# Giving each store of a preparation stage a place of its own among the projection matmuls

## The chip, the cores and the metric

The kernel runs on one core of one Trainium2 chip. The metric is the device time of one execution in microseconds (us); lower is better. Times of a kernel are given as the median of several runs. A profile is one execution recorded by the hardware profiler.

## The reference

One layer of a streaming encoder, for 512 tokens and 16 meta tokens (L = 528) of width 2048. All is float32.

```python
hn = _rmsnorm(h_res, norm_in_g[l])
P = hn @ w_in[l]                      # 2048 x 8320: r, k, v, g_r, lora | B, C, h, g_c
...
# group A: RWKV-7, 16 heads x 64, after a token shift of its columns
kk = (k * k_k[l]).reshape(bsz, L, H, N); kk = kk / norm(kk)
def step(S, inp):
    sa = jnp.einsum('bhvk,bhk->bhv', S, kk_t)
    S = (S * w_t[:, :, None, :] - sa[..., None] * b_t[:, :, None, :]
         + v_t[..., None] * k_t[:, :, None, :])
    y_t = jnp.einsum('bhvk,bhk->bhv', S, r_t)
...
y_a = (yn + bonus) * jax.nn.silu(g_r)                             # yn: GroupNorm of y
y_b = Bg * _causal_depthwise_conv(Cg * hc, conv_w[l]) * jax.nn.silu(g_c)   # group B
h_res = h_res + jnp.concatenate([y_a, y_b], axis=-1) @ w_out[l]
out = _rmsnorm(h_res, norm_f_g)                                   # meta tokens dropped
```

## The kernel before

**Projection.** The input projection is cut into 65 tiles of 128 output columns; `plan` (L105) lists them: lora, then for pair after pair of heads k, r, v, then g, C, h, B, gc. `main` (L323) is a generator that yields after each matmul, so that other work can be put between its matmuls. Full precision is kept by splitting every weight tile into a high and a low part: `prefetch` (L130) requests the 512 KB of half a tile (wr) on SyncE's queue, ScalarE casts it to the high part (wh, L126), and VectorE or GpSimd subtracts to give the low part (wl, L127). Three matmuls (high x high, high x low, low x high) then run per 128 rows. There are three wr buffers and six each of wh and wl.

**Preparation.** `prepare(i)`, for each of the 8 pairs of heads, turns k, r, v and the low-rank paths into the operands of a chunked form of the recurrence (9 chunks of 64 frames): ar, bk, the gram products gt (L625, masked by VectorE at L635), the transposes bt (L655) and vs. A small triangular system per chunk has to be inverted: its blocks go through DRAM (sg, L689) to another layout (d, L697), with the norms beside them (sn, L685, read back as nd, L698), VectorE inverts 16x16 blocks in a chain of some thirty small steps (the y chain, L701 to L734), y goes back through DRAM (sx, L749), and is loaded as xT and xo (L740, L741). `invert` joins two pairs on TensorE. All operands are stored to DRAM tensors opd by `stash` (L567): ar, gt (as O_KK and O_BR), bt (as O_B and O_K), vs (eight stores) and xT. They are read back chunk by chunk (ct, L870) only in `recur`, after all eight pairs. rbd (the bonus), gated (silu of g) and mixd (group B's result) are also stored, and read back by `split_mix` before the output projection (L1070), which takes the last 180 us or so.

**Order.** TensorE's order is written out by hand: the code calls `fill(ns)`, which takes matmuls of the projection from the generator until they fill that much time, and `until(...)`. The order on the other engines and on SyncE's queue is decided by a scheduler with a cost model, from the order of the program, dependences and priorities. `later(ns, fn)` (L482) puts a piece of work on a list that is due when the projection has run `ns` further; `run_pending` issues what is due, under `tc.issue_after(state["dma"])`, which keeps it on SyncE's queue behind the weight request that was issued last.

All these transfers are issued from one queue, SyncE's, in order; a request that waits holds up those behind it.

Of the kernel before, what the change touches and what calls it, by code (L numbers as in the profile page):

```python
# [18 lines left out]
P = 128  # L19
# [5 lines left out]
CH = 64  # L25
NCH = SEQ // CH + 1
# [12 lines left out]
O_AR, O_KK, O_BR, O_X, O_V, O_B, O_K = 0, 128, 256, 320, 384, 448, 512  # L39
# [37 lines left out]
def hymba_kernel(ctx: ExitStack, tc: tile.TileContext, xt, xtok, w_in, w_out, pv, lup, cst, msk, gf, out):  # L77
    nc = tc.nc
# [13 lines left out]
    rbd = [dp.tile([P, SEQ], F32, tag=f"rbd{j}", name=f"rbd{j}", bufs=1) for j in range(NPAIR)]  # L92
    gated = [dp.tile([P, SEQ], F32, tag=f"gated{j}", name=f"gated{j}", bufs=1) for j in range(NPAIR)]
    yd = dp.tile([2 * NPAIR * CH, SEQ], F32, tag="yd", name="yd", bufs=1)
    mixd = {j: dp.tile([P, SEQ], F32, tag=f"mixd{j}", name=f"mixd{j}", bufs=1) for j in range(NPAIR, KT)}
# [25 lines left out]
    state = {"next": 0}  # L121
# [255 lines left out]
    def use(what, i, ps):  # L377
        if what == "lora":
            use_lora(ps)
        elif what in ("k", "v"):  # L380
            t = cq.tile([P, LP], F32, tag=what, name=f"{what}{i}")
            nc.gpsimd.memset(t[:, META:CH], 0.0)
            shift_full(ps, tile_of[what] + i, f"{what}{i}", padded(t))
            got[what, i] = t
        elif what in ("r", "g"):
            t = cq.tile([P, SEQ], F32, tag=f"r{i % 2}" if what == "r" else "g", name=f"{what}{i}")
            shift_real(ps, tile_of[what] + i, f"{what}{i}", t)
            if what == "g":
                gate(t, f"r{i}")
                later(6000, lambda: nc.sync.dma_start(gated[i], t))  # L390
            got[what, i] = t
        elif what == "C":
            u = tm(f"u{i}")
            scaled(TAIL, ps, u, 14)
            got[what, i] = u
        elif what == "h":
            u = got["C", i]
            hh = tm(f"hh{i}")
            scaled(TAIL, ps, hh, 14)
            n = SEQ + 2  # L400
            nc.gpsimd.tensor_tensor(out=u[:, 0:n], in0=u[:, 0:n], in1=hh[:, 0:n], op=ALU.mult)
            cv = tp.tile([P, SEQ], F32, tag="cw", name=f"cv{i}")
            nc.scalar.activation(cv, u[:, 0:SEQ], AF.Copy, scale=col(V_CW, i))
            for j in (1, 2):
                nc.vector.scalar_tensor_tensor(
                    out=cv, in0=u[:, j : j + SEQ], scalar=col(V_CW, 8 * j + i), in1=cv, op0=ALU.mult, op1=ALU.add
                )
            got[what, i] = cv
        elif what == "B":
            cv = got["h", i]  # L410
            b = tm(f"b{i}")[:, 0:SEQ]
            scaled(REAL, ps, b, META)
            nc.gpsimd.tensor_tensor(out=cv, in0=cv, in1=b, op=ALU.mult)
        else:
            cv = got["h", i]
            g = tm(f"gc{i}")[:, 0:SEQ]
            scaled(REAL, ps, g, META)
            gate(g, f"c{i}")
            nc.vector.scalar_tensor_tensor(out=cv, in0=cv, scalar=0.5, in1=g, op0=ALU.mult, op1=ALU.mult)
            nc.sync.dma_start(mixd[8 + i], cv)  # L420
        ready.add((what, i))

    ready = set()
# [58 lines left out]
    def later(ns, fn):  # L482
        pending.append((clock[0] + ns, fn))
        pending.sort(key=lambda e: e[0])

    def run_pending(upto):
        while pending and pending[0][0] <= upto:
            fn = pending.pop(0)[1]
            with tc.issue_after(state["dma"]):
                fn()  # L490

    def step():
        t = next(flow, None)
        if t is None:
            run_pending(float("inf"))
        else:
            clock[0] += t
            run_pending(clock[0])
        return t
# [11 lines left out]
    def until(*key):  # L511
        while key not in ready:
            step()
# [41 lines left out]
    heads = [(h, slice(64 * h, 64 * h + 64), slice(64 - 64 * h, 128 - 64 * h)) for h in range(2)]  # L555
# [10 lines left out]
    def stash(i, src, o, n, row=0, rows_n=P, c0=0, cn=NCH, step=1):  # L566
        nc.sync.dma_start(spot(i, row, rows_n, c0, cn, step, o, n), src)  # L567

    def prepare(i):
        p = i % 2  # L570
        until("k", i)
        k = got["k", i]
        ar = cq.tile([P, NCH, 2, CH], F32, tag="ar", name=f"ar{i}")
# [32 lines left out]
        r = got["r", i]  # L606
# [13 lines left out]
        gt = cq.tile([P, 2, NCH, P], F32, tag=f"gt{p}", name=f"gt{i}")  # L620
# [56 lines left out]
        sx = scr_x[i % 2]  # L677

        def rows(t, h):
            return bass.AP(tensor=t.tensor, offset=t.offset + h * 4 * BLK, ap=[[CH, CH], [8 * BLK, NCH], [1, CH]])  # L680

        def blocks(t):
            return bass.AP(tensor=t.tensor, offset=t.offset, ap=[[BLK, 8 * NCH], [CH, 16], [1, 16]])

        nc.sync.dma_start(  # L685
            bass.AP(tensor=sn.tensor, offset=sn.offset, ap=[[CH, 2], [P, NCH], [1, CH]]), c3(n2[0:2])
        )
        for h in range(2):
            nc.sync.dma_start(rows(sg, h), gt[64 * h : 64 * h + 64, h, :, 0:CH])  # L689
        NB = 8 * NCH  # L690
        d = cq.tile([NB, 256], F32, tag="d", name=f"d{i}").rearrange("p (s t) -> p s t", t=16)
        stash(i, ar.rearrange("p c a s -> p c (a s)"), O_AR, 2 * CH)
        for h, hs, ho in heads:
            stash(i, gt[ho, h], O_KK, 2 * CH, 64 * h, 64)
            stash(i, gt[hs, h, :, CH:P], O_BR, CH, 64 * h, 64)
        nd = cq.tile([NB, 16], F32, tag="nd", name=f"nd{i}")
        nc.sync.dma_start(d, blocks(sg))  # L697
        nc.sync.dma_start(nd, sn.rearrange("(p s) -> p s", s=16))  # L698
        y = cq.tile([NB, 256], F32, tag="y", name=f"y{i}").rearrange("p (s t) -> p s t", t=16)
        nc.gpsimd.memset(y, 0.0)  # L700
        nc.vector.tensor_scalar(out=nd, in0=nd, scalar1=1e-24, scalar2=None, op0=ALU.max)  # L701
# [44 lines left out]
                    ),  # L746
                )

        later(13500 if p else 29000, lambda: nc.sync.dma_start(blocks(sx), y))  # L749
        later(16500 if p else 33000, load_inverse)  # L750

        for h, hs, ho in heads:
            stash(i, bt[hs, h], O_B, CH, 64 * h, 64, 0, NCH - 1)
            stash(i, bt[ho, h], O_K, CH, 64 * h, 64, 0, NCH - 1)
        until("v", i)
        v = got["v", i]
        nc.vector.tensor_tensor(out=r, in0=r, in1=v[:, CH:LP], op=ALU.mult)
        nc.sync.dma_start(rbd[i], r)
        fill(FW["v"])

        vs = cq.tile([P, NCH, CH], F32, tag="vs", name=f"vs{i}")
        nc.vector.transpose(vs.rearrange("p c s -> p (c s)"), v)
        for b in range(4):
            for t in range(2):
                stash(
                    i, vs[32 * b : 32 * b + 32, :, 32 * t : 32 * t + 32], O_V + 32 * (b % 2), 32,
                    64 * (1 - b // 2) + 32 * t, 32,
                )
        fill(FW["vt"])
# [2 lines left out]
    def invert(two):  # L772
# [81 lines left out]
        for q in both:  # L854
            for e in range(2):
                for h, lo, hi in quads:
                    nc.vector.tensor_copy(two[q]["xT"][lo, 2 - e : NCH : 2, 32:CH], z[e][lo, q])
        for t in two:
            if t["i"] % 2 == 0:
                stash(t["i"], t["xT"], O_X, CH)  # L860
            else:
                for h, hs, ho in heads:
                    stash(t["i"], t["xT"][hs], O_X, CH, 64 - 64 * h, 64)
        fill(FW["out"] if first < NPAIR - 2 else FW["begin"])

    def load_chunk(ch, c, pairs, ops):
# [128 lines left out]
    for i in range(0, NPAIR, 2):  # L995
        invert([prepare(i), prepare(i + 1)])
    until("g", NPAIR - 1)
    ph2.close()
    with tc.tile_pool(name="ch", bufs=1, side="right", reuse_waits="tile") as ch:
        recur(ch)  # L1000
# [5 lines left out]
    def split_mix(j):  # L1006
        parts[j] = [pp.tile([P, SEQ], F32R, name=f"m{a}{j}") for a in range(2)]
        mh, ml = parts[j]
        raw = pp.tile([P, SEQ], F32, tag="mraw", name=f"mr{j}", bufs=4)
        if j < NPAIR:  # L1010
            rb = pp.tile([P, SEQ], F32, tag="rb", name=f"rb{j}", bufs=3)
            gg = pp.tile([P, SEQ], F32, tag="gg", name=f"gg{j}", bufs=3)
            nc.sync.dma_start(rb, rbd[j])
            nc.sync.dma_start(gg, gated[j])
            for h, hs, ho in heads:
                o = ((1 - h if place[j] == NPAIR - 1 else h) * NPAIR + place[j]) * CH
                nc.sync.dma_start(raw[hs], yd[o : o + CH])

            for x, w, z, o in ((raw, 0, rb, ALU.mult), (raw, 1, gg, ALU.add)):
                nc.vector.scalar_tensor_tensor(  # L1020
                    out=raw, in0=x, scalar=hl[:, w, j : j + 1], in1=z, op0=o, op1=(ALU.add, ALU.mult)[w]
                )
        else:
            nc.sync.dma_start(raw, mixd[j])
        nc.scalar.copy(mh, raw)
        nc.vector.tensor_tensor(out=ml, in0=raw, in1=mh.bitcast(F32), op=ALU.subtract)
# [8 lines left out]
    for j in range(NPAIR + 4, KT):  # L1035
        while ("gc", j - NPAIR) not in ready:
            step()
        split_mix(j)
    for _ in flow:
        pass  # L1040
# [194 lines left out]
```

## Time and profile before

| | us |
|---|---|
| median of 3 runs | 1056.24 (1056.13 to 1057.02) |
| the profiled execution | 1054.6 |
| its span, first to last instruction | 1052.8 |
| TensorE busy | 1034.8 |
| VectorE busy | 566.4 |
| ScalarE busy | 365.9 |
| GpSimd busy | 308.3 |

The profile's rows name the engine (PE is TensorE, DVE VectorE, ACT ScalarE, POOL GpSimd, SPq SyncE's queue of DMA requests), the line of the kernel, what is written and what is read (out<-in), shapes, and how many instructions are merged in the row. The ends of matmuls are modelled, so a row of TensorE can overlap the next.

The stretches: startup to about 44 us, preparation and inversion of the pairs beside the projection to about 640, the recurrence beside the rest of the projection to about 800, the last of the projection to 865, the output projection to 1040, and the end.

### The profile page before, as it was taken

How to read it: one execution, taken by the hardware profiler on the slowest of the kernel's cores; microseconds unless marked ns; L12 is line 12 of the kernel's file. 1: busy time of each engine (PE TensorE's matmuls, PEld its weight loads, DVE VectorE, ACT ScalarE, POOL GpSimd, SP SyncE). 2: the span in 40 equal slices, each digit the busy share in tenths (PEclk: the TensorE clock that was granted, in tenths of full speed). 3: DMA queues.
4: the chain of work that ended last, by engine and by line, in shares of the span. 5: the costliest groups of instructions: out<-in, count | busy, mean ns of one | idle time of the engine just before them, and what ended most of it. 6: DMA issues, size and time to landing. Idle time of an engine off the chain costs nothing.

```text
span 1052.8 us, 23986 instructions
## 1 busy us (share of the span) xinstructions
PE 1034.8 (98%) x9973; PEld 945.1 (90%) x9973; DVE 566.4 (54%) x1072; ACT 365.9 (35%) x682; POOL 308.3 (29%) x315
## 2 busy tenths in 40 slices
PE   7999999999999999999999999999999999999996
PEld 6999998999998999989999989888898988888885
DVE  6774965559563658653757642455454781212132
ACT  7543422433332433233443232222222342323232
POOL 0132413324222323132323231323233242424232
PEclk9999999999999999999999999999999999999999
DMA  8446475364854363753364748778654978322314
GB/s 297 135 124 155 121 175 142 108 153 120 197 152 115 108 164 112 175 155 114 104 170 127 178 129 291 232 214 248 181 146 112 275 233 302 98 87 95 100 61 160
DMA packets 182893, 167.49 MB, mean 159 GB/s; under 512 B 120960, under 2 KB 143232, under 8 KB 182400
## 3 DMA queue, kind: packets, MB, share of 16 engines
q1 hardware_dynamic: 182208, 164.90, 53.7%
q8 instruction: 78, 1.28, 0.5%
q10 hardware_dynamic: 576, 1.07, 0.3%
q14 instruction: 31, 0.25, 0.1%
HBM read 129.05 MB, written 36.88 MB: 158 GB/s over the span
## 4 chain that ended last, share of the span: by engine, by line
PE 90%; DVE 4%; issue 2%; DMA 1%; ACT 1%; POOL 1%; SPq 0%; DVEq 0%; ACTq 0%; POOLq 0%
PE o L1070 17%; PE ps_g L315 9%; PE ps_gc L315 9%; PE ps_k L315 9%; PE ps_B L315 8%; PE ps_h L315 8%; PE ps_C L315 8%; PE ps_r L315 7%; PE ps_v L315 7%; PE g L625 2%; PE zs L939 1%; PE ps_lora L315 1%; PE rz L889 1%; PE zy L943 1%; DMA wq<-in_w_in_dram 1%
## 5 line engine op out<-in xcount | busy, mean ns | idle before, releaser
L127 POOL TENSOR_TENSOR wl<-wr,wh 128x512 fp32r<-128x512 f32 x150 | 211.2, 1410 | 456.2 <-ACT wh L126 423.2
L126 ACT CAST wh<-wr 128x512 fp32r<-128x512 f32 x312 | 188.7, 619 | 385.2 <-PE o L1070 92.2
L127 DVE TENSOR_TENSOR wl<-wr,wh 128x512 fp32r<-128x512 f32 x162 | 124.8, 775 | 241.4 <-ACT wh L126 236.0
L1070 PE MATMUL o<-wh,m 128*128 128x512 f32 (+1 forms) x484 | 145.3, 384 | 0.0
L1070 PEld LDWEIGHTS o<-wh,m 128*128 128x128 f32 x484 | 89.6, 188 | 21.3
L1070 PE MATMUL o<-wl,m 128*128 128x512 f32 (+1 forms) x242 | 92.6, 389 | 0.0
L315 PE MATMUL ps_k<-xl,wh 128*128 128x264 f32 x256 | 73.2, 286 | 0.0
L315 PE MATMUL ps_g<-xh,wl 128*128 128x258 f32 (+1 forms) x256 | 72.2, 282 | 0.9 <-DVE wl L127 0.8
L315 PE MATMUL ps_v<-xh,wh 128*128 128x264 f32 x256 | 73.1, 286 | 0.0
L315 PE MATMUL ps_k<-xh,wh 128*128 128x264 f32 x256 | 73.0, 285 | 0.0
L315 PE MATMUL ps_r<-xh,wh 128*128 128x258 f32 (+1 forms) x256 | 72.2, 282 | 0.7 <-ACT wh L225 0.7
L315 PE MATMUL ps_h<-xh,wl 128*128 128x258 f32 (+1 forms) x256 | 72.8, 285 | 0.0
L315 PE MATMUL ps_k<-xh,wl 128*128 128x264 f32 x256 | 72.7, 284 | 0.0
L315 PE MATMUL ps_v<-xh,wl 128*128 128x264 f32 x256 | 72.7, 284 | 0.0
L315 PE MATMUL ps_v<-xl,wh 128*128 128x264 f32 x256 | 72.7, 284 | 0.0
L315 PE MATMUL ps_g<-xl,wh 128*128 128x258 f32 (+1 forms) x256 | 72.4, 283 | 0.0
L315 PE MATMUL ps_h<-xh,wh 128*128 128x258 f32 (+1 forms) x256 | 72.3, 282 | 0.0
L315 PE MATMUL ps_g<-xh,wh 128*128 128x258 f32 (+1 forms) x256 | 72.3, 282 | 0.0
L315 PE MATMUL ps_C<-xh,wh 128*128 128x258 f32 (+1 forms) x256 | 72.3, 282 | 0.0
L315 PE MATMUL ps_C<-xh,wl 128*128 128x258 f32 (+1 forms) x256 | 72.3, 282 | 0.0
L315 PE MATMUL ps_r<-xl,wh 128*128 128x258 f32 (+1 forms) x256 | 72.1, 282 | 0.0
L315 PE MATMUL ps_h<-xl,wh 128*128 128x258 f32 (+1 forms) x256 | 72.1, 282 | 0.0
(271 smaller groups left out, 2705.9 us busy)
## 6 DMA issues: line engine op xcount, KB each, us to landing
wr<-in_w_in_dram SPq DMA_DIRECT2D x127, 512.0 KB
ct<-opd SPq DMA_DIRECT2D x64, 288.0 KB
wr<-in_w_out_dram SPq DMA_DIRECT2D x32, 512.0 KB
opd<-ar SPq DMA_DIRECT2D x8, 576.0 KB
opd<-gt SPq DMA_DIRECT2D x16, 288.0 KB
opd<-bt SPq DMA_DIRECT2D x32, 128.0 KB
xres<-in_xtok_dram SPq DMA_DIRECT2D x4, 768.0 KB
out_dram<-xres SPq DMA_DIRECT2D x6, 512.0 KB
```

What stands on the lines that cost most here:

```text
L126: nc.scalar.copy(hi, rq)
L127: eng.tensor_tensor(out=lo, in0=rq, in1=hi.bitcast(F32), op=ALU.subtract)
L315: nc.tensor.matmul(ps[r], ww[:, w], xx[:, kt, a:b], start=(kt == 0 and n == 0), stop=(kt == KT - 1 and n == 2))
L625: nc.tensor.matmul(z[h][:, c - c0], bk[hs, c, h : h + 2, :].rearrange("p a s -> p (a s)"), ar[hs, c].rearrange("p a s -> p (a s)"), start= ...
L889: nc.tensor.matmul(z[e][ho if e else hs, 0, k], t[hs, o : o + CH], t[hs, O_V : O_V + CH] if part else st[hs, 4 * e + k], start=(part == 0 ...
L939: nc.tensor.matmul(d[hs, j], t[hs, o : o + CH], x[hs], start=(a == 0), stop=(a == b - 1))
L943: nc.tensor.matmul(d[ho, j], t[hs, o : o + CH], x[hs], start=(a == 0), stop=(a == b - 1))
L1070: nc.tensor.matmul(ps[t + p], mm[:, tk], ww[:, o], start=(jj == 0 and q == 0), stop=(jj == KT - 1 and q == 2))
```

## The change

Every store of the preparation that went out where its data is produced gets a due time in the run of the projection (`stash_later`, `later`), so that it goes out behind the weight requested last by then. The solver's inputs (sg, sn, d, nd) are issued at once, but under `issue_after` (`behind`): they keep behind the weights requested before them. The write of y and the load of xT of odd pairs are due 7 and 6 us of projection later. The stores of xT (`put_inverse`), gated and mixd are due later too, and two calls of `run_pending` issue what is left before the recurrence and before the last loads of mixd.

```diff
-                later(6000, lambda: nc.sync.dma_start(gated[i], t))
+                later(14000, lambda: nc.sync.dma_start(gated[i], t))
...
-            nc.sync.dma_start(mixd[8 + i], cv)
+            later(9000, lambda: nc.sync.dma_start(mixd[8 + i], cv))
...
+    def behind(dst, src):
+        with tc.issue_after(state["dma"]):
+            nc.sync.dma_start(dst, src)
+    def stash_later(ns, *a):
+        later(ns, lambda: stash(*a))
...
-        nc.sync.dma_start(
+        behind(
             bass.AP(tensor=sn.tensor, offset=sn.offset, ap=[[CH, 2], [P, NCH], [1, CH]]), c3(n2[0:2])
         )
         for h in range(2):
-            nc.sync.dma_start(rows(sg, h), gt[64 * h : 64 * h + 64, h, :, 0:CH])
+            behind(rows(sg, h), gt[64 * h : 64 * h + 64, h, :, 0:CH])
...
-        stash(i, ar.rearrange("p c a s -> p c (a s)"), O_AR, 2 * CH)
+        stash_later(1500, i, ar.rearrange("p c a s -> p c (a s)"), O_AR, 2 * CH)
         for h, hs, ho in heads:
-            stash(i, gt[ho, h], O_KK, 2 * CH, 64 * h, 64)
-            stash(i, gt[hs, h, :, CH:P], O_BR, CH, 64 * h, 64)
+            stash_later(2500 + 1000 * h, i, gt[ho, h], O_KK, 2 * CH, 64 * h, 64)
+            stash_later(4500 + 1000 * h, i, gt[hs, h, :, CH:P], O_BR, CH, 64 * h, 64)
...
-        nc.sync.dma_start(d, blocks(sg))
-        nc.sync.dma_start(nd, sn.rearrange("(p s) -> p s", s=16))
+        behind(d, blocks(sg))
+        behind(nd, sn.rearrange("(p s) -> p s", s=16))
...
-        later(13500 if p else 29000, lambda: nc.sync.dma_start(blocks(sx), y))
-        later(16500 if p else 33000, load_inverse)
+        later(20500 if p else 29000, lambda: nc.sync.dma_start(blocks(sx), y))
+        later(22500 if p else 33000, load_inverse)
         for h, hs, ho in heads:
-            stash(i, bt[hs, h], O_B, CH, 64 * h, 64, 0, NCH - 1)
-            stash(i, bt[ho, h], O_K, CH, 64 * h, 64, 0, NCH - 1)
+            stash_later(6500 + 1000 * h, i, bt[hs, h], O_B, CH, 64 * h, 64, 0, NCH - 1)
+            stash_later(8500 + 1000 * h, i, bt[ho, h], O_K, CH, 64 * h, 64, 0, NCH - 1)
...
-        nc.sync.dma_start(rbd[i], r)
+        later(12500, lambda: nc.sync.dma_start(rbd[i], r))
...
-                stash(
-                    i, vs[32 * b : 32 * b + 32, :, 32 * t : 32 * t + 32], ...
+                stash_later(
+                    14000 + 1000 * (2 * b + t), i, vs[32 * b : 32 * b + 32, :, 32 * t : 32 * t + 32], ...
...
+        def put_inverse():
+            for t in two:
+                ...  # the stores of xT, as before
+        later(5500, put_inverse)
...
     until("g", NPAIR - 1)
+    run_pending(float("inf"))
...
+        run_pending(float("inf"))
         split_mix(j)
```

More of the change, by code (lines that the diff above doesn't have):

```diff
@@ L764, in prepare @@
             for t in range(2):
-                stash(
-                    i, vs[32 * b : 32 * b + 32, :, 32 * t : 32 * t + 32], O_V + 32 * (b % 2), 32,
+                stash_later(
+                    14000 + 1000 * (2 * b + t), i, vs[32 * b : 32 * b + 32, :, 32 * t : 32 * t + 32], O_V + 32 * (b % 2), 32,
                     64 * (1 - b // 2) + 32 * t, 32,
@@ L857, in invert @@
                     nc.vector.tensor_copy(two[q]["xT"][lo, 2 - e : NCH : 2, 32:CH], z[e][lo, q])
[L858 to L863, printed above, removed]
+        def put_inverse():
+            for t in two:
+                if t["i"] % 2 == 0:
+                    stash(t["i"], t["xT"], O_X, CH)
+                else:
+                    for h, hs, ho in heads:
+                        stash(t["i"], t["xT"][hs], O_X, CH, 64 - 64 * h, 64)
+        later(5500, put_inverse)
         fill(FW["out"] if first < NPAIR - 2 else FW["begin"])
```

## The prediction

> **What bounds the kernel now.** I read the page first: span, busy shares, the chain that ended last.
>
> ```profile
> span 1052.8 us, 23986 instructions
> ...
> PE 1034.8 (98%) x9973; PEld 945.1 (90%) x9973; DVE 566.4 (54%) x1072; ACT 365.9 (35%) x682; POOL 308.3 (29%) x315
> ...
> PE 90%; DVE 4%; issue 2%; DMA 1%; ACT 1%; POOL 1%; SPq 0%; DVEq 0%; ACTq 0%; POOLq 0%
> ```
>
> TensorE is busy for 98% of the span and carries 90% of the chain. The order of TensorE's instructions is written by hand and is, instruction for instruction, the same in the changed kernel. So no edit to a store can shorten TensorE's work; it can only remove, or add, pauses in it. I therefore went through TensorE's timeline start by start, from 44 us (the startup is over) to 640 us (the recurrence begins), which is the stretch in which the moved stores lie, and kept every place where the next start is late for its shape. There are four:
>
> ```profile
> 157.87 0.40 PE L315 MATMUL ps_B<-xh,wh 128*128 128x512 f32 x1
> 158.10 0.39 PE L315 MATMUL ps_B<-xl,wh 128*128 128x512 f32 x1
> 159.43 0.50 PE L315 MATMUL ps_B<-xh,wl 128*128 128x512 f32 x1 [0.94 <-DVE wl L127]
> ...
> 255.85 0.28 PE L315 MATMUL ps_g<-xh,wh 128*128 128x258 f32 x1
> 255.97 0.28 PE L315 MATMUL ps_g<-xl,wh 128*128 128x258 f32 x1
> 256.64 0.39 PE L315 MATMUL ps_g<-xh,wl 128*128 128x258 f32 x1 [0.39 <-DVE wl L127]
> 256.87 0.29 PE L315 MATMUL ps_g<-xh,wh 128*128 128x258 f32 x1
> ...
> 408.75 0.28 PE L315 MATMUL ps_g<-xl,wh 128*128 128x258 f32 x1
> 409.41 0.39 PE L315 MATMUL ps_g<-xh,wl 128*128 128x258 f32 x1 [0.38 <-DVE wl L127]
> ...
> 561.72 0.28 PE L315 MATMUL ps_g<-xl,wh 128*128 128x258 f32 x1
> 562.14 0.39 PE L315 MATMUL ps_g<-xh,wl 128*128 128x258 f32 x1
> ```
>
> The columns are start and duration; the bracket is idle time by the modelled end, so I count starts instead. A 128x512 step is 0.23 us (157.87 to 158.10), so 158.10 to 159.43 lost 1.10. A 128x258 step is 0.12 (255.85 to 255.97): the other three lost 0.55, 0.54 and 0.30. The first matmul after a pause also takes 0.11 longer to hand over (256.64 to 256.87 is 0.23). The sum is 2.49 + 4 x 0.11 = **2.9 us**, all the change can win here, and each time it is a weight's low part (wl, L127) on VectorE that came last.
>
> **The pause at 158 us.** Four engines show it, SyncE's queue first:
>
> ```profile
> 144.93 0.89 SPq L134 DMA_DIRECT2D wr<-in_w_in_dram  x2
> 154.05 1.30 POOL L401 TENSOR_TENSOR u<-u,hh 128x514 f32<-128x514 f32 x1 [11.04 <-DVE hh L334]
> 155.38 0.72 ACT L403 ACTIVATE cv<-u,pvt 128x512 f32<-128x512 f32 x1 [13.72 <-POOL u L401]
> 157.59 5.17 DVE L127 TENSOR_TENSOR wl<-wr,wh 128x512 fp32r<-128x512 f32 x3
> ```
>
> The weight tile wr23 is requested at 144.93, behind all the stores of pair 1; its cast stands on ScalarE behind the convolution's cv, which waits 13.72 us for a chain through VectorE and GpSimd. In the changed kernel's order wr23 stands in front of the four stores of bt, rbd and those of vs, and, because the scheduler now sees it early, its casts (wh46 to wh49) stand ahead of cv on ScalarE and wl46 inside the solver's y steps on VectorE, which begin at 142.06 (the nd row further down). That is well before 158. I take all of 1.10 + 0.11 as won. What covers it: the stores that moved behind are read back only in the recurrence, 480 us later.
>
> **The pauses at 256, 409 and 562 us.** These are one event in three rounds; I work out the first.
>
> ```profile
> 222.51 1.28 SPq L689 DMA_DIRECT2D sg<-gt  x2
> 229.93 2.09 SPq L698 DMA_DIRECT2D nd<-sn  x1
> 239.16 1.34 SPq L134 DMA_DIRECT2D wr<-in_w_in_dram  x3
> ...
> 232.04 0.44 DVE L334 TENSOR_TENSOR pr_k<-ps_k,rs 128x264 f32<-128x264 f32 x1 [1.02 <-PE ps_k L315]
> 233.28 1.38 DVE L343 SCALAR_TENSOR_TENSOR k<-pr_k,omm,sh_k 128x16 f32<-128x16 f32 x2 [0.81 <-ACT sh_k L341]
> 236.32 0.17 DVE L701 TENSOR_SCALAR nd<-nd 72x16 f32<-72x16 f32 x1
> 246.60 0.76 DVE L601 TENSOR_TENSOR ta<-ta,k 128x576 f32<-128x576 f32 x1 [0.67 <-POOL ta L595]
> 251.65 0.69 DVE L607 TENSOR_TENSOR ar<-r,e 128x512 f32<-128x512 f32 x1
> 253.51 1.16 DVE L728 TENSOR_TENSOR prod<-y,tt 72x512 f32<-72x512 f32 x1
> 254.71 0.68 DVE L734 TENSOR_REDUCE y<-prod 72x64 f32<-72x512 f32 x1
> 255.91 1.28 DVE L127 TENSOR_TENSOR wl<-wr,wh 128x512 fp32r<-128x512 f32 x2
> ...
> 259.62 1.99 PE g L625 x32
> ```
>
> Here wr38, 39 and 40 leave at 239.16, after the solver's inputs (sg, sn, d, nd) and all stores of pair 2, and the first wl of wr38 comes on VectorE at 255.91, when TensorE already waits. In the new order wr38 follows the solver's loads after two stores of gt, and its wl stands ahead of the last two steps of the solver's chain. The pause goes if nothing else becomes late. What becomes late is pair 3's own preparation: VectorE now takes nd right after pr_k, the whole y chain next, and te, bk, ta and ar behind it, while TensorE's gram (L625) needs ar. Old order: nd at 236.32 to the end of ar at 252.34, 16.0 us, its 0.67 wait in it. New order: in the same stretch also the three last y steps (0.68 + 1.16 + 0.68 = 2.5; the first is as long as the last), k (1.4) and three weight splits (3 x 0.64 = 1.9): 16.0 + 2.5 + 1.4 + 1.9 = 21.8, and I add 0.2 for the cast between r and ar: **22.0 us from nd to ar**. The gram would start at 259.62 - 0.66 = 258.96. So nd must be there by **236.9**.
>
> When is it? In the new order d directly follows the two sg stores and one store of gt, and nd follows sn by one store, so SyncE waits on landings which four stores covered before. Rows for a store that is read back, and for a load of nd:
>
> ```profile
> 294.18 0.32 SPq L749 DMA_DIRECT2D sx<-y  x1
> 296.65 0.60 SPq L740 DMA_DIRECT2D xT<-sx  x1
> ...
> 122.27 0.35 SPq L749 DMA_DIRECT2D sx<-y  x1
> 126.82 0.61 SPq L740 DMA_DIRECT2D xT<-sx  x1
> ...
> 138.41 1.00 SPq L698 DMA_DIRECT2D nd<-sn  x1
> 142.06 0.98 DVE L701 TENSOR_SCALAR nd<-nd 72x16 f32<-72x16 f32 x1 [0.53 <-DMA nd<-sn]
> ```
>
> From a store's issue to the read that waits for it: 2.5 us in a quiet queue, 4.5 in a full one. The second sg leaves at 223.1; d at 225.6 (227.6); it takes 1.0 to issue like nd, and sn leaves at 226.6 (228.6); nd at 229.1 (233.1); it is usable 3.65 later (138.41 to 142.06): **232.8, at worst 236.8**. I take 232.8, by the quiet row, since here no xT loads are under way as at 122 us. Up to 232.48 VectorE still has pr_k to do, so the wait costs it nothing, ar ends at 254.8, 4.1 us before the gram, and at the worst end still 0.1 before it. wr38 then leaves near 232 to 236 instead of 239.16: the SyncE waits sit ahead of it, but fewer stores do.
>
> A rule of the Trainium skill speaks against this step: DMA: Bandwidth & Descriptors, section Anatomy of one DMA, says that DMA engines do not wait on semaphores, the issuing sequencer does, and puts the fixed cost of one DMA near 2.0 us, most of it the receipt of the write. By it, d and nd each hold SyncE's queue, weights included, for an estimated 2 us; the quiet row above (2.47) agrees, and the sum would stay the same.
>
> **The other edits.** The odd rounds (pair 3, 5, 7) get vs, rbd and gated behind weights, and xT 6 us later by the plan; xT is still issued before the transposes, so nothing waits. mixd (L420) and the stores of xT (put_inverse) keep their places on SyncE up to the recurrence, and the ct loads keep theirs behind them, so those lines of the diff change nothing: 0, and TensorE's pauses in the recurrence stay. The extra run_pending calls find nothing urgent. No bytes are added or removed.
>
> **The sum.** The profiled execution took 1054.6 us (span 1052.8 and 1.8 around it); the median of three runs is 1056.24. I subtract 2.9 from both: 1051.7 for a profile, **1053.3 us** for the median, 0.27% less. A measurement of this kernel can tell about 0.2%, 2.1 us, from no change.
>
> **Rivals.** *One: the won time is given back in part, no change.* For pair 1 the preparation of pair 0's solver is also pulled ahead, and the masks of the gram, which were just in time, come after it:
>
> ```profile
> 100.82 1.68 POOL L581 TENSOR_SCALAR tz<-tz 128x576 f32<-128x576 f32 x1 [2.72 <-ACT tz L528]
> ...
> 104.45 1.34 DVE L583 TENSOR_TENSOR_SCAN cc<-smask,tz 128x576 f32<-128x576 f32 x1
> 124.90 2.48 DVE L635 TENSOR_TENSOR gt<-g,cs 128x512 f32<-128x512 f32 x4
> ...
> 127.87 0.49 PE L625 MATMUL g<-ar,bk 64*128 64x128 f32 x4
> ```
>
> The masks end at 127.38, TensorE needs them at 127.87. From cc to there VectorE works 22.9 us; the new order adds a wl and a pr_v (1.1) and about 0.3 of waiting on ScalarE's casts of g: 24.3. If cc starts as soon as tz is there (102.5) the masks end at 126.8, in time; if it starts at 104.45 as now, at 128.75, a new pause of 0.9. With nd 0.4 past its limit in three rounds (1.2) as well: 1056.24 - 2.9 + 0.9 + 1.2 = 1055.4. For it: both margins are thin at their bad ends. Against: nd of pair 0 arrives earlier too.
>
> *Two: slower, VectorE stuck at nd.* VectorE takes its instructions in order (so does ScalarE: cv above held the casts for 13.72). If nd lands after 236.9, k, cc, te, bk and ar all stand behind it, and each us past that costs TensorE one us in each of three rounds. It outweighs the gain from 237.9 on. At 239.3 (2.4 us late, three waits of 4.5 with another load's traffic on top): 1056.24 - 2.9 + 3 x 2.4 = 1060.5. For it: SyncE now waits twice in a row there. Against: it needs more than the worst row of this trace at every step. The Trainium skill (TensorE: Matmul & The Clock Gate, section Architectural detail) calls ACT and DVE strict FIFO, which the cv row bears out; it changes no number here.
>
> **How the numbers follow.** Forecast 0.57, rival one 0.23, rival two 0.17, the rest (a larger gain because the recurrence's pauses shift too) 0.03. Faster by over 0.2% takes the forecast less 0.03 for a stall only partly gone, and the rest: 0.57. Slower by over 0.2% is rival two less 0.02: 0.15. Within 0.2% is what is left, 0.28. The range goes from 1052.3 (1 us more than the four pauses, leaving out 0.05) to 1057.8, through rival one and the lower half of rival two, leaving out about 0.1.
>
> **What would show it.** Right: in the profile after, no wait of ps_B or ps_g for wl; the gram of pair 3 about 0.66 + 1.21 us earlier than 259.62; nd on VectorE near 233; wr38 requested before 237. Wrong: TensorE waiting for ar, gt or wl somewhere between 100 and 640 us, or an idle of VectorE before nd of more than 4 us.

## The result and the profile after

| | before | after |
|---|---|---|
| median of 5 runs each, us | 1056.13 (1055.13 to 1057.02) | 1051.63 (1051.32 to 1052.75) |
| the profiled execution, us | 1054.6 | 1052.52 |
| its span, us | 1052.8 | 1050.6 |

The ratio is 0.9961, with a 95% interval of 0.9946 to 0.9975: 2.6 to 5.7 us less. The direction and the place are as forecast. The size is not: 1051.63 lies below the low end of the range, 1052.3. The interval taken alone still holds the forecast 2.9 us; whether the gain is 2.9 or 4.5 had to come from the runs below. The two profiled executions differ by only 2.1 us, the medians by 4.5.

The page of the changed kernel, and its waits of TensorE (us in total, times, longest):

```profile
span 1050.6 us, 23971 instructions
...
PE 1034.6 (98%) x9973; PEld 945.3 (90%) x9973; DVE 568.7 (54%) x1072; ACT 366.5 (35%) x682; POOL 303.7 (29%) x315
...
PE 96%; DMA 2%; DVE 1%; SPq 1%; issue 0%; ACT 0%; POOL 0%; DVEq 0%; ACTq 0%
```

```profile
PE ps_lora L315 <- DVE xl L190: 1.8, 3, 1.0
PE rz L951 <- issue: 1.6, 1, 1.6
PE pwarm L175 <- DVE cold L172: 1.4, 1, 1.4
PE zy L955 <- issue: 1.3, 1, 1.3
PE ps_lora L315 <- ACT xh L189: 0.9, 2, 0.7
PE ps_r L315 <- ACT wh L225: 0.7, 1, 0.7
```

TensorE's busy time is the same within 0.2 us; the chain is 96% TensorE instead of 90%. No wait for wl is left, and none in 44 to 640 us: what remains belongs to the startup (ps_lora, ps_r, pwarm) and the recurrence (rz, zy). At the place of the second pause the starts now follow each other in 0.12 us. This and the next fence are the changed kernel's timeline (start, duration):

```profile
255.21 0.28 PE L315 MATMUL ps_g<-xh,wh 128*128 128x258 f32 x1
255.33 0.28 PE L315 MATMUL ps_g<-xl,wh 128*128 128x258 f32 x1
255.45 0.28 PE L315 MATMUL ps_g<-xh,wl 128*128 128x258 f32 x1
```

```profile
225.05 0.33 SPq L571 DMA_DIRECT2D d<-sg  x1
...
227.51 0.30 SPq L571 DMA_DIRECT2D nd<-sn  x1
...
229.23 1.08 SPq L134 DMA_DIRECT2D wr<-in_w_in_dram  x1
...
231.74 0.16 DVE L709 TENSOR_SCALAR nd<-nd 72x16 f32<-72x16 f32 x1
...
244.95 0.68 DVE L127 TENSOR_TENSOR wl<-wr,wh 128x512 fp32r<-128x512 f32 x1
...
254.79 0.68 DVE L615 TENSOR_TENSOR ar<-r,e 128x512 f32<-128x512 f32 x1
...
258.28 2.06 PE L633 MATMUL g<-ar,bk 64*128 64x128 f32 x32
```

wr38 leaves at 229.23 instead of 239.16, and the first low part of it stands on VectorE at 244.95 instead of 255.91. VectorE takes nd without a wait at 231.74, ar ends at 255.47, and the gram has 2.8 us to spare.

The four stretches of projection that held the pauses (one B tile, and three times the two g tiles of two pairs) now take 11.11, 27.11, 27.11 and 27.12 us, against 12.32, 27.70, 27.97 and 27.44: 2.98 us less, the 2.9 of the sum. The changed kernel's profile left the startup 0.56 us later and lost 0.34 more at 748 us, which is how 2.98 became a span shorter by 2.2. So this pair of profiles agrees with the sum and leaves the median's other 1.5 us unexplained. That is what the experiments had to find.

### The profile page after: what moved, and what is told of

It reads as the page before. It is cut to its first block, busy times and chain, and to the rows that moved or that the text cites. A ratio compares the mean times of both kernels' runs of the same rounds, so it can differ in the third digit from the quotient of the medians.

```text
span 1050.6 us, 23971 instructions
## 1 busy us (share of the span) xinstructions
PE 1034.6 (98%) x9973; PEld 945.3 (90%) x9973; DVE 568.7 (54%) x1072; ACT 366.5 (35%) x682; POOL 303.7 (29%) x315
## 4 chain that ended last, share of the span: by engine, by line
PE 96%; DMA 2%; DVE 1%; SPq 1%; issue 0%; ACT 0%; POOL 0%; DVEq 0%; ACTq 0%
PE o L1084 17%; PE ps_v L315 9%; PE ps_h L315 9%; PE ps_g L315 9%; PE ps_gc L315 9%; PE ps_k L315 9%; PE ps_B L315 9%; PE ps_r L315 8%; PE ps_C L315 8%; PE g L633 2%; PE zs L951 1%; DMA wq<-in_w_in_dram 1%; PE ps_lora L315 1%; PE rz L901 1%; PE zy L955 1%; DMA ct<-opd 1%
## 5 line engine op out<-in xcount | busy, mean ns | idle before, releaser
L127 POOL TENSOR_TENSOR wl<-wr,wh 128x512 fp32r<-128x512 f32 x150 | 204.4, 1363 | 474.7 <-ACT wh L126 436.8
L127 DVE TENSOR_TENSOR wl<-wr,wh 128x512 fp32r<-128x512 f32 x162 | 117.9, 730 | 230.2 <-ACT wh L126 222.9
L315 PE MATMUL ps_C<-xl,wh 128*128 128x258 f32 (+1 forms) x256 | 72.1, 282 | 0.0
```

The lines of the kernel that those rows point to most:

```text
L127: eng.tensor_tensor(out=lo, in0=rq, in1=hi.bitcast(F32), op=ALU.subtract)
L315: nc.tensor.matmul(ps[r], ww[:, w], xx[:, kt, a:b], start=(kt == 0 and n == 0), stop=(kt == KT - 1 and n == 2))
```

## The experiments

Theory one: the pauses of the kernel before differ between executions, and the profiled one had less than most. Theory two: executions differ for reasons the change doesn't touch. Theory three: a gain outside 44 to 640 us. Between them stand the parts of the change, run alone.

### Both kernels once more

No edit to either.

> The kernel before, once more, to see what differs between two executions of it. Its own ratio should be 1 within 0.1%. Theory one (the pauses of the weights' low parts are larger in other executions than in the one that was profiled): the starts of TensorE between 44 and 640 us are late by 3.5 to 5 us in sum, not 2.49. Theory two (the pauses are always the same, and executions differ by up to 1 us for reasons that the change does not touch, such as the startup or the granted clock): the same four pauses, 2.4 to 2.6 us in sum, and what differs lies before 50 us or is spread over the span. Theory three (a gain outside 44 to 640 us that the first pair of profiles did not show): some pause after 640 us is here larger than in the first profile.

> The changed kernel, once more. Theory one: again 4.5 us less than the kernel before (ratio 0.9957), and no pause in 44 to 640 us. Theory two: the gain of 4.5 us was partly the luck of the sample, the gain is the 2.9 to 3.0 us of the pauses, ratio 0.9971 to 0.9973. Theory three: again 4.5 us, and some stretch after 640 us is shorter than in the kernel before, by 1 to 1.5 us.

The changed kernel again had 0.9957 of the time before (0.9944 to 0.9969), 1053.08 against 1057.57, and its four stretches took the same to 0.01 us. The kernel before, against itself, had 0.9994 (0.9983 to 1.0006). Its second profile showed three of the four pauses as before, one shorter (0.51 at 159 us), and a new one: at 573 us the gram of pair 7 waited 0.55 for its masks, 0.71 by starts. Theory two had expected 0.9971 to 0.9973, which lies outside the interval: it falls for the larger part. Theory three found little: tile by tile, no stretch of TensorE behind 640 us is shorter in both profiles of the changed kernel than in both of the kernel before. Only the end behind the last matmul is, by 0.25 us (8.13 against 8.38); what makes it so wasn't followed up. Two profiles were too few for theory one.

### Stores alone, solver's part alone

```diff
 stores_only:  def behind(dst, src):
-    with tc.issue_after(state["dma"]):
-        nc.sync.dma_start(dst, src)
+    nc.sync.dma_start(dst, src)
-later(20500 if p ...)   -later(22500 if p ...)
+later(13500 if p ...)   +later(16500 if p ...)
 solver_only:  the kernel before, with behind() for sn, sg, d, nd
+later(20500 if p ...)   +later(22500 if p ...)
```

> The stores of the preparation, rbd, vs, gated, mixd and xT have their due times, but the solver's inputs (sn, sg, d, nd) go out where they stand in the program and the write of y and the load of xT keep their old due times. By the forecast's steps the stores ahead of wr23 and wr38 are the cause of all four pauses, and keeping the solver's inputs behind requested weights is not: no pause for wl in 44 to 640 us, and the same gain as the whole change (2.9 by the sum, 4.5 if theory one or three of the changed kernel holds). Rival: the solver's inputs ahead of the weight keep the three later pauses, 1.4 us of the gain goes, 1.5 is left.

> The other part alone: the solver's inputs keep behind the requested weights and the write of y and the load of xT of odd pairs are due later, but every store goes out where its data is produced, as before. By the forecast's steps: no gain, all four pauses stay (2.4 to 2.6 us in sum), 1056 us. Rival (the solver's inputs are what holds the weights up): the three later pauses go, 1.7 us less.

stores_only: 0.9953 (0.994 to 0.9967), no pause in 44 to 640 us. The stores carry the whole gain, as far as the interval tells.

solver_only: 1068.1 us, ratio 1.0106 (1.0087 to 1.0124), 11 us slower, which neither theory expected. `behind` alone was not run. But in this profile SyncE's queue differs from that of the kernel before only around the write of y, the loads of xT and xo and the requests beside them (31 of 604 places); sn, sg, d and nd keep theirs. So the loss belongs to the later due times. The timeline and the windows of solver_only (columns: stretch, its length, busy time of five engines, then the granted clock, DMA share, GB/s):

```profile
310.31 0.69 PE L806 MATMUL t<-xn,gt 64*64 64x64 f32 x32 [3.10 <-DVE xn L799]
```

```profile
308.00:312.00 4.00, 1.69 (x35) 1.50 (x36) 1.14 (x2) 0.96 (x2) 0.46 (x1) 0.89 0.32 86
312.00:316.00 4.00, 4.00 (x13) 2.92 (x11) 1.11 (x2) 1.37 (x3) 2.07 (x2) 0.69 0.43 127
```

xT comes 3 us later (its first load leaves at 300.27 instead of 296.65), the transposes xn wait for it, TensorE waits 3.1 us for them, and then the clock falls: 128x512 steps take 0.43 us instead of 0.23 for 3.4 us. That is 4.9 us in this round (two tiles: 16.07 and 13.91 instead of 12.69 and 12.40) and 12.8 over three.

### Early pairs alone, later pairs alone

```diff
+def new(i):
+    return i < 2        # first_pairs;  later_pairs: i >= 2
 # stash_later, behind, rbd, put_inverse and the due times as changed where new(i), else as before
```

> The change for pairs 0 and 1 alone; pairs 2 to 7 are handled as before (gated and mixd as in the changed kernel). By the forecast's steps the pause at 158 us goes and the three others stay: 1.21 us less than the kernel before (ratio 0.9989). If the unexplained 1.5 us of the whole change come from rounds that were not disturbed in the first profile (theory one, the gt masks behind a late low part of a weight, as at 573 us in the second execution of the kernel before), the gain here is still 0.6 to 1.2, and the rest comes with the later pairs. Theory two (executions differ by things the change does not touch): both halves scale alike, here 1.2 x 4.5 / 2.9 = 1.9.

> The change for pairs 2 to 7 alone. By the forecast's steps: the pause at 158 us stays (0.5 to 1.2), the other three go, 1.7 us less (ratio 0.9984). Theory one: 3 to 3.5 us less (ratio 0.9967 to 0.9972), since the late masks of the gram belong to these rounds too. Theory two: 2.6 us less.

first_pairs: 0.9987 (0.9975 to 0.9998), 1.4 us less. later_pairs: 0.9965 (0.9952 to 0.9979), 3.7 us less. The first interval is too wide to tell 1.21 from 1.9, but in its profile the stretch at 158 us is back at the 11.11 us of the changed kernel. The second (2.2 to 5.1 us) lies above the forecast's 1.7 for the later pairs. But in the profile of later_pairs the pause at 158 us was 0.30 instead of 1.10, and with some 0.7 us from there neither the forecast's 1.7 nor theory two's 2.6 is shut out by the time alone. Theory one, a missing part in pairs 3, 5 and 7, fits; the profiles have to decide. In first_pairs, whose later pairs are handled as before, the gram waited for its masks twice, 1.29 at 266 us and 0.52 at 573.

### More executions of the kernel before

No edit, one profile each.

> A third execution of the kernel before, for its pauses alone. Theory one: besides the four pauses for wl there are one or more waits of the gram's last chunk for the masks gt (0.7 us each, as at 573 us in the second execution), at 267, 420 or 573 us; sum over 44 to 640 us above 2.5 us. Theory two: 2.4 to 2.7 us in sum without such waits.

> A fourth execution of the kernel before, as the third. If theory one holds, the four executions have sums between 2.5 and 5 us with a mean near 4; if theory two holds, all four lie between 2.4 and 2.7.

> A fifth execution of the kernel before, for its pauses alone. The four so far, tile by tile against the changed kernel, lost 2.99, 3.97, 4.80 and 3.97 us in the four rounds, two of them with a wait of the gram for its masks. If such waits are the missing 1.5 us, the executions to come lie between 3 and 6 us, their mean is 4.0 to 4.5, and one in three or four of the rounds of pairs 3, 5 and 7 has such a wait. If not, they lie at 2.9 to 3.2 and the missing part is at the granted clock.

> A sixth execution of the kernel before, as the fifth. Where a wait for masks occurs, the cast of the weight requested just before (near 259, 412 or 565 us) should have waited for its landing for over 5 us from the request, against 3.8 where there is no wait.

> A seventh execution of the kernel before, as the fifth. By the clock theory a stretch at half clock should stand in 44 to 640 us, behind one of the pauses, in some of these executions; by the theory of the masks there is none.

> An eighth execution of the kernel before, as the fifth: three to six us lost in the four rounds if waits for masks are the missing part, 2.9 to 3.2 if not.

For each execution, what the four stretches lost against the changed kernel's (its two profiles and that of stores_only agree to 0.01 us), and the pauses of the gram for its masks, by starts:

| execution of before | lost in four stretches, us | waits for masks (at us) |
|---|---|---|
| the first profile | 2.98 | none |
| second (copy_before) | 3.96 | 0.71 (573) |
| b | 4.79 | 1.41 (267) |
| c | 3.96 | none |
| d | 5.89 | 1.65 (267), 0.42 (575) |
| e | 4.72 | 0.35 (419), 0.47 (572) |
| f | 7.43 | 1.85 (268), 0.16 (577) |
| g | 4.46 | 0.52 (573) |

The mean is 4.77 us and the median 4.6, beside the 4.5 measured; the profile from which the forecast was made is the lowest of eight. The four wl pauses stand in all eight with nearly the same length (0.53 to 0.59 at 256 and 409, 0.29 to 0.32 at 562; at 158 it was 1.08 to 1.10 in seven and 0.51 in one). What varies is the wait for the masks: 9 of 24 rounds have one ahead of the group of gram and bt matmuls. More of the loss lies inside that group, where the waits view shows nothing: from the step before it to the step behind it, near 419 us, it took 1.13 us in the changed kernel, 1.44 in the first profile and 1.65 in c. Split by place against the changed kernel, the mean of 4.77 us is 2.72 up to the group (the wl pauses), 0.84 ahead of the group's first matmul, 1.11 inside the group and 0.10 behind it.

Where it comes from is seen by following one weight, in the first profile and in f:

```profile
259.31 1.55 SPq L134 DMA_DIRECT2D wr<-in_w_in_dram  x2
...
263.11 0.62 ACT L126 CAST wh<-wr 128x512 fp32r<-128x512 f32 x1 [3.80 <-DMA wr<-in_w_in_dram]
...
263.76 0.69 DVE L127 TENSOR_TENSOR wl<-wr,wh 128x512 fp32r<-128x512 f32 x1 [0.67 <-ACT wh L126]
264.37 2.48 DVE L635 TENSOR_TENSOR gt<-g,cs 128x512 f32<-128x512 f32 x4
...
266.95 0.49 PE L625 MATMUL g<-ar,bk 64*128 64x128 f32 x4
```

```profile
260.17 1.55 SPq L134 DMA_DIRECT2D wr<-in_w_in_dram  x2
...
266.35 1.14 ACT L126 CAST wh<-wr 128x512 fp32r<-128x512 f32 x2 [6.18 <-DMA wr<-in_w_in_dram]
...
267.00 0.69 DVE L127 TENSOR_TENSOR wl<-wr,wh 128x512 fp32r<-128x512 f32 x1 [3.04 <-ACT wh L126]
267.61 2.75 DVE L635 TENSOR_TENSOR gt<-g,cs 128x512 f32<-128x512 f32 x5
...
269.55 0.97 PE L625 MATMUL g<-ar,bk 64*128 64x128 f32 x3 [1.69 <-DVE gt L635]
```

The weight is requested only at 259.31 (260.17), because its buffer comes free that late: GpSimd's wl, which reads the buffer, ends at 259.28 (260.15). ScalarE casts it as soon as it lands, 3.80 or 6.18 us after the request. On VectorE its low part stands ahead of the four masks, and TensorE's gram of the last chunk writes to the buffers that the last two of them read: its first head needs the third mask, its second head the fourth. In the first profile the fourth mask ended 0.10 before the gram (264.37 + 2.48 = 266.85, against 266.95): no pause, but no spare time either. In c, near 419 us, the third was in time and the fourth was not (the first row is VectorE's timeline up to 419.46):

```profile
416.97 2.48 DVE L635 TENSOR_TENSOR gt<-g,cs 128x512 f32<-128x512 f32 x4
...
418.97 0.91 PE L625 MATMUL g<-ar,bk 64*128 64x128 f32 x3
419.51 0.27 PE L655 MATMUL bt<-cs,bk 64*128 64x64 f32 x1
```

The fourth mask ended at 419.45. The gram's first head had started at 418.97; its second head, third of the x3 in the row, started only at 419.50, and bt behind it. TensorE's modelled ends overlap there, so no idle time is listed. This is so in 21 of the 24 rounds: the second head started 0.05 to 0.14 us behind the end of the fourth mask.

Over the 24 rounds the request-to-cast time runs from 3.74 to 6.18 us. Up to 4.37 there is no wait ahead of the group; the nine above it (4.49 to 6.18) paused for that time less 4.33, each within 0.06 us. The delay of the whole group, the part inside it included, is that time less 3.85, within 0.05 us in all 24 (none where the time was shorter). So one cause accounts for the 0.84 and the 1.11. The expectation of "over 5 us" was too high a threshold: it is 4.4 for a wait ahead of the group, 3.85 for any delay.

In the changed kernel the same place has no cast that waits for a landing:

```profile
259.99 0.60 ACT L126 CAST wh<-wr 128x512 fp32r<-128x512 f32 x1
...
261.75 0.65 DVE L127 TENSOR_TENSOR wl<-wr,wh 128x512 fp32r<-128x512 f32 x1
262.32 2.47 DVE L643 TENSOR_TENSOR gt<-g,cs 128x512 f32<-128x512 f32 x4
...
265.69 0.49 PE L633 MATMUL g<-ar,bk 64*128 64x128 f32 x4
```

The weight has been there since before ScalarE came to it, the masks end 0.9 us ahead of the gram, and its three rounds take the same time in every profile.

In f the pause also cost clock, as the clock theory had it (windows of f):

```profile
272.00:274.00 2.00, 2.00 (x11) 2.00 (x11) 0.69 (x1) 0.74 (x2) 0.00 (x0) 0.50 0.86 200
274.00:276.00 2.00, 2.00 (x15) 2.00 (x15) 0.43 (x1) 0.00 (x0) 0.00 (x0) 0.72 1.13 301
```

That is 1.5 of its 7.43 us, once in eight executions, so some 0.2 of the mean.

### Margins, and other parts

```diff
 d_3x (changed kernel):
-behind(d, blocks(sg))
+for _ in range(3):
+    behind(d, blocks(sg))
 late_due (changed kernel):
-later(20500 if p ...)   -later(22500 if p ...)
+later(23500 if p ...)   +later(25500 if p ...)
 vs_only (kernel before): rbd and the eight stores of vs through later(), due as changed,
   and the run_pending call before the recurrence
 rest_only (kernel before): gated, mixd and put_inverse due as changed, run_pending as changed
```

> The changed kernel, with the load of d issued three times in place of once, ahead of nd, in every pair. It tests step four of the forecast, the spare time of VectorE between nd and the gram of pair 3. In the changed kernel nd is taken up at 231.74, the last ar ends at 255.47 and the gram starts at 258.28: 2.8 us are left. Each extra load waits for the one before it (2.5 to 3.3 us), so nd comes 5 to 6.5 us later. By the forecast's rule (each us past the limit costs TensorE one us in three rounds): 2 to 4 us late, 6 to 12 us more than the changed kernel, less where other work of VectorE slips in ahead of nd. Rival (nd is not what VectorE's chain hangs on, the work behind it moves ahead): within 1 us of the changed kernel.

d_3x: 0.9962 (0.9948 to 0.9975), as the changed kernel within the noise; the rival holds in the main. Its timeline:

```profile
231.20 0.72 SPq L571 DMA_DIRECT2D nd<-sn  x1
...
234.96 0.16 DVE L710 TENSOR_SCALAR nd<-nd 72x16 f32<-72x16 f32 x1
...
256.29 0.68 DVE L615 TENSOR_TENSOR ar<-r,e 128x512 f32<-128x512 f32 x1
...
259.30 2.06 PE L633 MATMUL g<-ar,bk 64*128 64x128 f32 x32
```

nd is requested 3.7 us later and used 3.2 later, yet ar keeps 2.3 us before the gram (2.8 in the changed kernel): the scheduler put k, 1.4 us, ahead of nd, and about 1 us is that all of TensorE runs later there (0.5 from the startup, 0.5 lost at 129 us). It wasn't quite free. In its profile the second head of the gram started just behind the fourth mask in all four odd pairs: the groups took 0.53 us longer at 129 us and 0.18 to 0.24 in the three later rounds, 1.1 in sum. The expectation counted extra landings one after the other at 2.5 us or more; d was in fact issued at 226.32, 228.62 and 230.86.

> The kernel before, with due times for the stores of vs and for rbd alone (nine of the seventeen stores of a pair); ar, gt and bt go out at once. The pauses come from weights that stand behind a run of stores. If what counts is the length of the run, the weight wr38 leaves some 3.5 to 4.5 us earlier than 239.16, which is more than the pauses of 0.3 to 1.1 us: all four go, and the gain is that of the whole change, 4.5 us (ratio 0.9957). If the order that the scheduler gives VectorE decides (the low part of the weight ahead of the last steps of the solver's chain), about half of it is left, 1.5 to 2.5 us.

vs_only: 0.995 (0.9934 to 0.9967). Nine stores of a pair are enough. (A pair has eighteen of these, not seventeen: one of ar, four of gt, four of bt, eight of vs, and rbd.) wr38, 39 and 40 leave like this (SyncE's queue):

```profile
232.56 0.57 SPq L134 DMA_DIRECT2D wr<-in_w_in_dram  x1
...
233.73 0.35 SPq L134 DMA_DIRECT2D wr<-in_w_in_dram  x1
...
239.09 0.33 SPq L134 DMA_DIRECT2D wr<-in_w_in_dram  x1
```

The first of them gains 6.6 us, not 3.5 to 4.5, and every wl pause goes. One round still waits for its masks: 0.16 us ahead of the group, 0.64 with the part inside it.

> The kernel before, with the later due times of gated, mixd and the stores of xT and the two extra calls that flush the list, and none of the rest. The forecast puts these edits at 0: ratio 1 within 0.1%, all four pauses there. Rival: the stores of xT hold up weights as the others do, and a part of the later pairs' gain, 1 us or more, comes from here.

rest_only: 0.9987 (0.9974 to 1.0). The profile shows all four pauses (0.30, 0.54, 0.54, 0.30) and a wait for masks of 0.24; its stretches lost 3.35 us, within the spread of the kernel before. So 0 fits, at the edge of the interval; a gain of 1.4 us, or by the interval up to 2.7, isn't excluded. The first pause was 0.30 here, as in later_pairs, instead of the 1.10 of seven executions of the kernel before. The later gated and mixd are common to these two runs, so they may shorten it by some 0.7 us; that wasn't tested further, and copy_before had a pause of 0.51 without them.

> The changed kernel, with the write of y and the load of xT of odd pairs due another 3 us of projection later (23500 and 25500). The later due times alone, on the kernel before, cost 11 us: the transposes xn waited up to 3.1 us for xT in three rounds, and TensorE ran some 4 us at a lower clock behind each. If the changed kernel has the room because its stores no longer stand in front of xT (in it xT leaves at 297.35, against 300.27 there): no change, within 1 us of the changed kernel. If it stands close to the edge: xT leaves near 300.3 and the same pauses come, 9 to 12 us more.

late_due: 1067.69, ratio 1.0088 (1.0069 to 1.0108), some 14 us more than the changed kernel. The changed kernel stands close to the edge where xT comes too late. Its own timeline, then that of late_due with two of its windows:

```profile
297.35 0.60 SPq L748 DMA_DIRECT2D xT<-sx  x1
...
304.27 0.70 DVE L793 STREAM_TRANSPOSE xn<-xT 128x512 f32<-128x512 f32 x1
```

```profile
303.12 1.80 SPq L748 DMA_DIRECT2D xT<-sx  x1
...
308.96 0.71 DVE L793 STREAM_TRANSPOSE xn<-xT 128x512 f32<-128x512 f32 x1 [3.52 <-DMA xT<-sx]
...
309.73 0.69 PE L800 MATMUL t<-xn,gt 64*64 64x64 f32 x32 [2.83 <-DVE xn L793]
```

```profile
310.00:312.00 2.00, 2.00 (x34) 1.65 (x25) 0.43 (x1) 1.08 (x2) 0.93 (x1) 0.59 0.00 0
312.00:314.00 2.00, 2.00 (x7) 1.56 (x6) 0.00 (x0) 0.38 (x1) 1.58 (x2) 0.56 0.38 47
```

A due time 3 us later moves xT by 5.8 us, since two weight requests come in front of it; xn waits 3.52 and TensorE 2.83, and the clock drops again.

## Why the prediction was right in its mechanism and wrong in its size

**TensorE bound, order unchanged: right.** Only pauses moved.

**The pause at 158 us: right.** 1.21 won in the profile; first_pairs alone measured 0.2 to 2.6 us, which agrees but says little.

**The pauses at 256, 409 and 562 us: right for the pauses seen.** d left at 225.05 (forecast 225.6), nd at 227.51 (229.1), wr38 at 229.23 (232 to 236, so earlier than forecast); nd was there when VectorE came to it. From nd to the end of ar it took 23.7 us instead of 22.0, so 2.8 us were spare and not 4.1. The gram of pair 3 came 1.27 us earlier in the timeline, 1.83 with the later startup taken off (forecast 1.87).

**The step that failed: "the sum is ... 2.9 us, all the change can win here".** The pauses of one execution were taken for the pauses of the kernel, and were then subtracted from a median of others. Eight executions lost 4.77 us on average, 2.98 to 7.43. The term put at nothing is the gram's wait for its masks behind a weight that has just landed, which cost 1.95 us on average (0.84 ahead of the group, 1.11 inside it). In the profile that I had it was 0.32, hidden inside the group at 419 us, and it was there to be seen as a place with 0.10 us to spare behind a transfer. That this profile's 2.98 agrees with 2.9 is partly luck: the wl pauses were 2.8 of it. I searched for late starts and not for starts that were only just on time. That the profiled execution (1054.6) was below all three runs shown (1056.13 to 1057.02) was a sign of it, and I noted it and subtracted from both alike. With 4.77 the sum is 1051.5; measured 1051.63; so close an agreement is partly luck, given the spread of the eight. The low end, 1 us beyond the sum, was too near for the same reason.

**Other edits cost nothing: right for the changed kernel, on a thin margin.** "xT is still issued before the transposes, so nothing waits" took the issue for the landing. The later due times cost 11 us without the moved stores, and 14 with 3 us more. `behind`, mixd and put_inverse showed no part clear of the noise; for gated and mixd up to 1.4 us stays open (rest_only).

**Rival one: not seen in the changed kernel.** The masks of pair 1 ended at 126.60, the gram took them at 128.43, and nd wasn't late. In d_3x it came in a mild form: the fourth mask ended at 129.35, the gram's second head started at 129.41, and the group took 0.53 us longer. **Rival two: not seen.** d_3x shows that a late nd also needn't hold k up: the scheduler reorders around it.

**The rest, 0.03 ("a larger gain because the recurrence's pauses shift too"):** the gain was larger, but not for that; rz and zy stay.

## What to carry to other kernels

A queue's order is worth looking at where a request for the bottleneck's input stands behind a run of transfers that nobody needs soon; moving nine of eighteen stores was enough here. In a profile, list also the places where a just-landed transfer feeds the bottleneck with almost no time to spare: they were the pauses of the next executions. A list of waits misses the ones that hide under overlapping instructions; lengths of whole tiles, compared between executions, show them. Before a pause is subtracted from a median, profile the kernel several times.

## What the runs showed of the hardware

The same request of a weight, in the same place of the same program, was cast 3.74 to 6.18 us after its issue. What makes one landing slower than another isn't shown.

A pause of TensorE can cost more than its length. In solver_only and late_due the six waits for xn were 2.05 to 3.37 us long, and behind each of them the granted clock fell to half. In f it did so after 1.69 us (1.85 by starts); behind the mask waits of 1.26 and 1.49 us, in b and d, it didn't. The Trainium skill (TensorE: Matmul & The Clock Gate, section HAM oscillation — how this bites in real kernels) gives as its rule that there should be no idle gaps above about 3.4 us; here shorter ones were enough. Whatever the pause, the stretch at half clock lasted 3.4 us, in all 17 cases of the 18 profiles (these seven and the ten below).

In the recurrence the pause of rz, for which the profile names no releaser, was 1.61 to 2.09 us, in all 18 profiles. In 10 of 18 profiled executions the clock fell to half behind it: the projection tile around it took 19.65 to 20.15 us there, 18.14 to 18.58 in the other eight. The length of the pause didn't decide: 1.73 us was followed by half clock in solver_only, 2.05 in stores_only was not. Here c:

```profile
728.76 0.27 PE L939 MATMUL rz<-u,ct 64*64 64x64 f32 x2 [2.01 <-issue]
```

```profile
730.00:732.00 2.00, 2.00 (x11) 2.00 (x10) 1.20 (x6) 0.63 (x1) 0.00 (x0) 0.50 0.97 350
```

Neither kernel's first profile had it; four of the eight of the kernel before had it, and one of the two of the changed kernel. It is a part of the spread of single runs. Nothing suggests that the change touches it, but two profiles are too few to show that; why the pause is there stays open.
